# A hybrid Mamba-2 and attention trunk: step sizes by fp32 products, decay differences on ScalarE, sums in two half buffers

## The chip, the cores and the metric

The kernel runs on one core of a Trainium2 chip. The metric is the device time of one execution in microseconds. Engines are named as in the profile: PE (TensorE products) and PEld (its weight loads), DVE (VectorE), ACT (ScalarE), POOL (GpSimd) and SP (SyncE, which issues most DMAs).

## The reference, cut to what matters

The trunk has two layers on x of 256 tokens by 2048 channels: a Mamba-2 SSD mixer, then sliding-window attention. All of it is float32. The change lies in the first mixer:

```python
zxbcdt = x @ w_in                      # 2048 x (4096 z + 6144 xbc + 64 dt)
xbc = silu(conv4(xbc) + conv_b)        # xs (64 heads x 64), B and C (8 groups x 128)
dt = softplus(dt_raw + dt_bias)        # one step size per token and head
a = -exp(a_log)
# chunks of 128 tokens; s is the running sum of dt * a
y = sum over t <= q of (C[q] . B[t]) * exp(s[q] - s[t]) * (xs[t] * dt[t]) + xs * d_skip
y = rmsnorm_by_group(y * silu(z)) * norm_w
x = layernorm(alpha * x + y @ w_out)   # then the attention layer on this x
```

## The kernel before, in words

**Splits.** A float32 product on PE is made of three products of split halves: each weight block is loaded raw (`wr`), ACT writes its rounded half `wh` (L133), DVE the rest `wl` (L134), and PE adds wh·xH, wh·xL and wl·xH (L195 to L197, `mac`). x is split in the same way into xH and xL. A block ("unit") is 2048 by 128 weights, loaded as two halves of 512 KB; five raw buffers and four of each split half stand in turn, and loading runs two units ahead (`next_unit`, L179). In the SSD layer a block's 48 products of 128x128 by 128x256 fill one PSUM tile `mm` of four.

**Order of the work.** SSD heads go in eight groups. A group has ten projection blocks: B, C, four of xs, four of z (group 0 takes z first). Output products of the group before are put between them. A plan (`at`, L581 on) hangs the other steps behind a block number: `load_decay`, `sum_decay`, `exp_decay`, `cb` (C·B and the mask, multiplied into the decays), `tr` (transposes of xs), `ymm` (products with the decays), `gate`, `norm`. A scheduler then settles the order on each engine's queue, in which instructions stay in order; some steps get a priority (`high_priority`).

**The start.** `load_first` (L136) loads eight pieces of 1 to 3 k-tiles of 512 columns: 256 of x, 128 of the step-size block, 128 of block 0 (z). The step-size weights stand there twice, so that rows 0 to 63 and 64 to 127 of the product are the same 64 heads. `gemm_ws` (L282) makes both products, piece by piece. `make_dt` (L299) turns the first into dt by a series on DVE, splits dt·a into a coarse part (rows 0 to 63) and a rest (rows 64 to 127), and runs both sums along the tokens in one scan (L326); the sums go to DRAM (`rscr`, L327). `turn_dt` transposes the sums and dt on PE (L333, L334).

**Decays.** `load_decay` (L366) reads four heads' coarse and low sums back, broadcast to all 128 partitions (`rb`, one buffer, two loads of 512 KB). `sum_decay` (L378) makes on DVE, for each head, coarse[q] − coarse[t] + low[q] in two ops (L384, 256 columns; L388, 128 columns), then one minimum with 80 over all four heads (L392). `exp_decay` (L395) is one exp on ACT (L397). The low sum of t goes into dt (`dtx`). `ymm` (L453) multiplies the decays with xd on PE (L468: fp32, 64 columns, two halves of the array) and DVE adds xs·d_skip straight from PSUM (L475).

Of the kernel before, what the change touches and what calls it, by code (L numbers as in the profile page):

```python
# [28 lines left out]
NFIRST = 2  # L29
FIRST = [(0, 1), (1, 2), (2, 4), (4, 6), (6, 9), (9, 12), (12, 14), (14, 16)]  # L30
# [27 lines left out]
def trunk(ctx: ExitStack, tc: tile.TileContext, A: dict, out: bass.AP, dbg=None):  # L58
# [60 lines left out]

    def load_unit(src, places):  # L120
        u = new_unit(places)
        raws = []
        for c in range(2):
            raw = wp.tile([P, 1024], F32, tag="wr", name=nm("wr"), bufs=NR)
            nc.sync.dma_start(raw[:], src[:, c * 1024 : (c + 1) * 1024])
            raws.append(raw)
        for c in range(2):
            for (h, k0, k1), (l, _, _) in zip(*u.parts):
                a, b = max(k0, 8 * c), min(k1, 8 * c + 8)
                if a < b:  # L130
                    sl = slice((a - k0) * P, (b - k0) * P)
                    raw = raws[c][:, (a - 8 * c) * P : (b - 8 * c) * P]
                    nc.scalar.activation(h[:, sl], raw, AF.Copy)  # L133
                    nc.vector.tensor_tensor(l[:, sl], raw, h[:, sl].bitcast(F32), ALU.subtract)  # L134
        return u

    def load_first():

        us = [new_unit([WHOLE, WHOLE]) for _ in range(2)]
        for k0, k1 in FIRST:  # L140
            n = k1 - k0
            if n < 3:
                raw = wp.tile([P, 2, 512], F32, tag="wr", name=nm("first"), bufs=NR)
            else:
                raw = ap.tile([P, 3, 512], F32, tag="e", name=nm("first"), bufs=2)
            raw = raw[:, :n, :]
            nc.sync.dma_start(raw, A["first"][:, k0:k1, :])
            nc.scalar.activation(xH(k0, k1), raw[:, :, :S], AF.Copy)
            nc.vector.tensor_tensor(xL(k0, k1), raw[:, :, :S], xH(k0, k1).bitcast(F32), ALU.subtract)
            for i, u in enumerate(us):  # L150
                h, l = [p[:, k0 * P : k1 * P].rearrange("p (k c) -> p k c", c=P) for p in (u.h, u.l)]
                w = raw[:, :, S + i * P : S + (i + 1) * P]
                nc.scalar.activation(h, w, AF.Copy)  # L153
                nc.vector.tensor_tensor(l, w, h.bitcast(F32), ALU.subtract)
        return us


    srcs = [None]
# [20 lines left out]
    def next_unit():  # L179
        if not units:  # L180
            units.extend(load_first())
            nc.sync.dma_start(pc[:], A["pc"])
        while len(units) < min(used[0] + 1 + AHEAD, len(srcs)):
            if len(units) == 5:
                nc.sync.dma_start(cc[:], A["cc"])
            if len(units) in (8, 9):
                i = len(units) - 8
# [6 lines left out]
    def mac(ps, ah, al, bh, bl, first, last):  # L194
        nc.tensor.matmul(ps, ah, bh, start=first, stop=False)  # L195
        nc.tensor.matmul(ps, ah, bl, start=False, stop=False)  # L196
        nc.tensor.matmul(ps, al, bh, start=False, stop=last)  # L197
# [29 lines left out]
    class Split:  # L227


        def __init__(self, name, first, at0, at1):  # L230
            gap = (at1 - at0) % 256 // 4
            t = ap.tile([P, KT * S + 128], F32R, tag=name, name=name)
# [49 lines left out]
    def gemm_ws(us):  # L282
        pss = [mm_tile() for _ in us]
        for k0, k1 in FIRST:
            for ps, u in zip(pss, us):
                for k in range(k0, k1):
                    ks = slice(k * P, (k + 1) * P)
                    mac(
                        ps[:, :S], u.h[:, ks], u.l[:, ks], xH(k, k + 1)[:, 0, :], xL(k, k + 1)[:, 0, :],
                        k == 0, k == KT - 1,  # L290
                    )
        return pss
# [6 lines left out]
    def make_dt(ps):  # L299
        f = [ap.tile([P, S], F32, tag="sm", name=nm("f"), bufs=NSM) for _ in range(7)]  # L300
        u, e, rec, z, w, q, dt = [x[:] for x in f]
        nc.scalar.activation(u, ps[:, :S], AF.Identity, bias=pc[:, PC_DTB : PC_DTB + 1])
# [24 lines left out]
        nc.sync.dma_start(rscr[:], rc)  # L327
# [37 lines left out]

    def load_decay(g, hf):  # L366
        rb = ap.tile([P, 2, 4, S], F32, tag="rb", name=nm("rb"), bufs=1)
        h0 = g * 8 + hf * 4
        for part in range(2):
            nc.sync.dma_start(  # L370
                rb[:, part, :, :],
                rscr[part * 64 + h0 : part * 64 + h0 + 4, :]
                .rearrange("h q -> (h q)").partition_broadcast(P)
                .rearrange("p (h q) -> p h q", h=4),
            )
        rbs[g, hf] = rb

    def sum_decay(g, hf):  # L378
# [16 lines left out]
    def exp_decay(g, hf):  # L395
        e = es[g, hf]
        nc.scalar.activation(e[:], e[:], AF.Exp)  # L397
# [58 lines left out]
    def ymm(g):  # L456
        st = gs[g]
        st.yz = ap.tile([P, 4, S], F32, tag="yz", name=nm("yz"), bufs=1)
        for k in range(2):
            ps = ax_tile()  # L460
            for i in (2 * k, 2 * k + 1):
                o = (i % 2) * S
                xd = st.xd[i]
                for c in range(2):
                    cols = slice(o + c * P, o + S)
                    for r in range(2):
# [4 lines left out]
                        )  # L471
# [547 lines left out]
```

## Time and profile before

| | |
|---|---|
| runs, us | 1023.79, 1024.12, 1253.01 (median 1024.12) |
| profiled execution, us | 1023.71 |
| its span, us | 1021.9 |
| mean granted PE clock | 0.997 |
| busy PE / DVE / ACT / POOL, us | 1002.5 / 806.3 / 521.7 / 84.9 |
| DMA | 203.5 MB, 199 GB/s over the span |
| wh splits on ACT (L133), us | 338.0 |
| wl splits on DVE (L134), us | 393.5 |
| decay sums and minimum on DVE (L384, L388, L392), us | 36.2 + 24.5 + 15.2 |
| exp of decays on ACT (L397), us | 23.9 |
| landing of rb, median from issue, us | 4.8 |

Busy time is the union of an engine's instructions; a matmul's end is modelled and matmuls overlap, so the distance between the starts of two of them tells more than their durations. A row of a group gives busy time, mean duration, then the idle time of the engine just before, and who ended it. Names read out<-in, and shapes partitions by elements.

### The profile page before, as it was taken

Reading aid. Unit: us, or ns where it says so; the run is one execution under the profiler, and the core shown is the slowest. Engines: PE = TensorE matmul, PEld = TensorE weight load, DVE = VectorE, ACT = ScalarE, POOL = GpSimd, SP = SyncE. Lnnn points to the kernel's source line nnn. Section 1 sums busy time; section 2 is a strip of 40 time slices with the busy share of each in tenths; the row PEclk is TensorE's granted clock in tenths of the full one; section 3 lists DMA queues with packets and bytes.
Section 4 is the critical chain, followed back from the end, with each engine's and each line's share of the span. In section 5 each row is a group of like instructions: output and inputs, shape, how many; then the busy total and the mean of one; then the engine's idle time right before and its main releaser. Section 6 shows DMA issues by size and latency. Waiting matters only on the chain. (4 is left out here: it accounts for less than half of the span.)

```text
span 1021.9 us, 17613 instructions
## 1 busy us (share of the span) xinstructions
PE 1002.5 (98%) x7028; PEld 906.6 (89%) x7028; DVE 806.3 (79%) x1234; ACT 521.7 (51%) x795; POOL 84.9 (8%) x112
## 2 busy tenths in 40 slices
PE   7999999999999999999999999999999999999997
PEld 7998999999998998999999999878988878879975
DVE  6889897886895995986897797798577785785776
ACT  6565554744654554564464474535545453453642
POOL 0000303003003001100300300301000000000002
PEclk9999999999999999999999999999999999999999
DMA  8887585674764765666567466646555445545522
GB/s 307 281 301 241 167 270 176 226 235 141 260 212 143 266 202 192 213 208 219 178 207 239 159 196 229 241 145 234 195 167 170 154 142 182 173 142 182 193 97 82
DMA packets 55730, 203.50 MB, mean 199 GB/s; under 512 B 6288, under 2 KB 6560, under 8 KB 54880
## 3 DMA queue, kind: packets, MB, share of 16 engines
q1 hardware_dynamic: 54288, 196.33, 57.2%
q0 software_dynamic: 1072, 5.53, 1.6%
q8 instruction: 55, 0.90, 0.4%
q10 hardware_dynamic: 288, 0.52, 0.1%
q14 instruction: 27, 0.22, 0.1%
HBM read 200.13 MB, written 2.23 MB: 198 GB/s over the span
## 5 line engine op out<-in xcount | busy, mean ns | idle before, releaser
L134 DVE TENSOR_TENSOR wl<-wr,wh 128x1024 fp32r<-128x1024 f32 (+2 forms) x342 | 393.5, 1169 | 103.0 <-ACT wh L133 101.5
L133 ACT ACTIVATE wh<-wr 128x1024 fp32r<-128x1024 f32 (+2 forms) x342 | 338.0, 1012 | 230.8 <-PE mm L196 67.2
L195 PE MATMUL mm<-xH,wh 128*128 128x256 f32 x1296 | 361.7, 279 | 7.8 <-ACT wh L153 6.0
L197 PE MATMUL mm<-xH,wl 128*128 128x256 f32 x1296 | 360.3, 278 | 3.1 <-DVE wl L134 3.1
L196 PE MATMUL mm<-xL,wh 128*128 128x256 f32 x1296 | 360.7, 279 | 0.0
L195 PEld LDWEIGHTS mm<-xH,wh 128*128 128x128 f32 x1296 | 245.3, 189 | 9.8 <-ACT wh L153 6.3
L197 PEld LDWEIGHTS mm<-xH,wl 128*128 128x128 f32 x1296 | 245.2, 189 | 3.6 <-DVE wl L134 3.5
L196 PEld LDWEIGHTS mm<-xL,wh 128*128 128x128 f32 x1296 | 245.4, 189 | 1.1
L255 PE MATMUL mm<-wh,yH 128*128 128x512 f32 x256 | 101.4, 396 | 0.0
L256 PE MATMUL mm<-wh,yL 128*128 128x512 f32 x256 | 99.9, 390 | 0.0
L257 PE MATMUL mm<-wl,yH 128*128 128x512 f32 x256 | 99.7, 390 | 0.0
L482 POOL TENSOR_TENSOR yz<-yz,z 128x256 f32<-128x256 f32 x32 | 29.8, 931 | 538.5 <-DVE yz L475 538.5
L195 PE MATMUL mm<-x1H,wh 128*128 128x256 f32 x256 | 71.9, 281 | 0.0
L197 PE MATMUL mm<-x1H,wl 128*128 128x256 f32 x256 | 71.0, 277 | 0.0
L196 PE MATMUL mm<-x1L,wh 128*128 128x256 f32 x256 | 71.0, 277 | 0.0
L356 DVE SCALAR_TENSOR_TENSOR cv<-mm,pc,cv 128x255 f32<-128x255 f32 x144 | 68.6, 476 | 2.5 <-ACT cv L354 1.6
L704 PE MATMUL mm<-wh,x1H 128*128 128x512 f32 x160 | 63.3, 396 | 0.0
L706 PE MATMUL mm<-wl,x1H 128*128 128x512 f32 x160 | 62.7, 392 | 0.2 <-DVE wl L134 0.2
L705 PE MATMUL mm<-wh,x1L 128*128 128x512 f32 x160 | 62.7, 392 | 0.2 <-DVE x1L L668 0.2
L255 PEld LDWEIGHTS mm<-wh,yH 128*128 128x128 f32 x256 | 48.1, 188 | 10.3 <-DVE z L421 0.9
L257 PEld LDWEIGHTS mm<-wl,yH 128*128 128x128 f32 x256 | 48.1, 188 | 10.1
L256 PEld LDWEIGHTS mm<-wh,yL 128*128 128x128 f32 x256 | 48.1, 188 | 9.0
(181 smaller groups left out, 1308.5 us busy)
## 6 DMA issues: line engine op xcount, KB each, us to landing
wr<-in_wa SPq DMA_DIRECT2D x158, 512.0 KB, 5.2
wr<-in_wo SPq DMA_DIRECT2D x64, 512.0 KB, 5.3
rb<-rscr SPq DMA_DIRECT2D x32, 512.0 KB, 4.8
wr<-in_wq SPq DMA_DIRECT2D x32, 512.0 KB, 4.5
wr<-in_wg SPq DMA_DIRECT2D x32, 512.0 KB, 5.3
wr<-in_wb SPq DMA_DIRECT2D x32, 512.0 KB, 4.6
wr<-in_wkv SPq DMA_DIRECT2D x8, 512.0 KB, 6.6
first<-in_first SPq DMA_DIRECT2D x4, 512.0 KB, 8.8
```

Source lines behind the costliest of these rows:

```text
L133: nc.scalar.activation(h[:, sl], raw, AF.Copy)
L134: nc.vector.tensor_tensor(l[:, sl], raw, h[:, sl].bitcast(F32), ALU.subtract)
L195: nc.tensor.matmul(ps, ah, bh, start=first, stop=False)
L196: nc.tensor.matmul(ps, ah, bl, start=False, stop=False)
L197: nc.tensor.matmul(ps, al, bh, start=False, stop=last)
L255: nc.tensor.matmul(ps[:], aH[:, k, hs], u.h[:, ks], start=k == 0, stop=False)
L256: nc.tensor.matmul(ps[:], aL[:, k, hs], u.h[:, ks], start=False, stop=False)
L257: nc.tensor.matmul(ps[:], aH[:, k, hs], u.l[:, ks], start=False, stop=k == 3)
L356: nc.vector.scalar_tensor_tensor(a[:, sft:], ps[:, : S - sft], w(3 - sft), a[:, sft:], ALU.mult, ALU.add)
L704: nc.tensor.matmul(ps[:], x1H[:, kk, hs], u.h[:, ks], start=kk == 0, stop=False)
L705: nc.tensor.matmul(ps[:], x1L[:, kk, hs], u.h[:, ks], start=False, stop=False)
L706: nc.tensor.matmul(ps[:], x1H[:, kk, hs], u.l[:, ks], start=False, stop=kk == KT - 1)
```

## The change

Four things are altered.

1. The step sizes come from 16 fp32 products of 64 columns, straight from the raw pieces, with no split. Even k go to PSUM rows 0 to 63, odd k to rows 64 to 127; `make_dt` adds the two halves with two ACT copies across partitions and one DVE op. The pieces hold 448 columns. Block 1 is loaded in two halves among the pieces, and products of the step sizes and blocks 0 and 1 are pinned to the order in `ORDER`. Raw pieces are now read by PE too, so their buffers come free later; the last one borrows a buffer of `rb`.
2. The decay differences are made on ACT: Relu(coarse[t] − coarse[q]), and the exp takes them with scale −1. The minimum on DVE is gone.
3. The low sum of q is left out of the difference. Its exp is taken once in `make_dt`, stored, loaded for a group as `el` (two loads of 64 partitions), and multiplied on DVE into ymm's result (128x512), before xs·d_skip is added in SBUF.
4. `rb` is two buffers of half the size, with only the coarse sums, and the plan loads both halves together; sums and exps stand at other block numbers. The pc scaling goes behind `make_dt`.

```diff
+FIRST = [(0, 1), (1, 2), (2, 4), (4, 6), (6, 8), "h0", (8, 11), (11, 14), (14, 16), "h1"]
+ORDER = [(0, 0, 1), (1, 0, 2), (0, 1, 4), (1, 2, 6), (0, 4, 8), (1, 6, 8), (2, 0, 8), (0, 8, 14), (1, 8, 14),
+         (0, 14, 16), (1, 14, 16), (2, 8, 16)]
+FW = 256 + 128 + 64
...
+        for piece in FIRST:
+            if isinstance(piece, str):
+                c = int(piece[1])
+                split_half(us[1], load_half(us[1], A["wa"][1], c), c)
+                continue
...
+            if k0 == 14:
+                raw = ap.tile([P, 4 * S], F32, tag="rb", name=nm("first"), bufs=2)
+            elif n < 3:
+                raw = wp.tile([P, 1024], F32, tag="wr", name=nm("first"), bufs=NR)
             else:
-                raw = ap.tile([P, 3, 512], F32, tag="e", name=nm("first"), bufs=2)
+                raw = ap.tile([P, 1536], F32, tag="e", name=nm("first"), bufs=2)
...
+    def first_products():
+        us, raws = load_first()
+        units.extend(us)
+        nc.sync.dma_start(pc[:], A["pc"])
+        pss = [mm_tile() for _ in range(3)]
+        for i, k0, k1 in ORDER:
+            if i:
+                narrow(pss[i], us[i - 1], k0, k1, True)
+                continue
+            for k in range(k0, k1):
+                r = 64 * (k % 2)
+                tc.keep_in_program_order(
+                    nc.tensor.matmul(
+                        pss[0][r : r + 64, :S], raws[k][:, S + P :], raws[k][:, :S], start=k < 2, stop=k >= KT - 2
+                    )
                 )
...
-        nc.scalar.activation(u, ps[:, :S], AF.Identity, bias=pc[:, PC_DTB : PC_DTB + 1])
+        for r in (0, 64):
+            nc.scalar.copy(e[r : r + 64], ps[64 - r : 128 - r, :S])
+        nc.vector.scalar_tensor_tensor(u, ps[:, :S], pc[:, PC_DTB : PC_DTB + 1], e, ALU.add, ALU.add)
...
-        nc.sync.dma_start(rscr[:], rc)
+        nc.sync.dma_start(rscr[0:64, :], rc[:64])
+        nc.scalar.activation(hi[64:128], rc[64:128], AF.Exp)
+        nc.sync.dma_start(rscr[64:128, :], hi[64:128])
...
     def load_decay(g, hf):
-        rb = ap.tile([P, 2, 4, S], F32, tag="rb", name=nm("rb"), bufs=1)
+        rb = ap.tile([P, 4, S], F32, tag="rb", name=nm("rb"), bufs=2)
...
+    def load_low(g):
+        el = ap.tile([P, 4, S], F32, tag="el", name=nm("el"), bufs=1)
+        rows = rscr[64 + g * 8 : 64 + g * 8 + 8, :].rearrange("(i r) q -> r i q", r=2)
+        for r in range(2):
+            nc.sync.dma_start(el[64 * r : 64 * r + 64, :, :], rows[r].partition_broadcast(64))
+        els[g] = el
...
         for h in range(4):
-            nc.vector.scalar_tensor_tensor(
-                e[:, h, :256], rb[:, 0, h, :], rtk[:, 0, h0 + h : h0 + h + 1], rb[:, 1, h, :],
-                ALU.subtract, ALU.add,
-            )
-            nc.vector.scalar_tensor_tensor(
-                e[:, h, 256:], rb[:, 0, h, 128:], rtk[:, 1, h0 + h : h0 + h + 1], rb[:, 1, h, 128:],
-                ALU.subtract, ALU.add,
-            )
-        nc.vector.tensor_scalar(e[:], e[:], 80.0, None, ALU.min)
+            for c, cols in ((0, slice(0, 256)), (1, slice(256, 384))):
+                nc.scalar.activation(
+                    e[:, h, cols], rb[:, h, c * P :], AF.Relu, scale=-1.0, bias=rtk[:, c, h0 + h : h0 + h + 1]
+                )
...
-        nc.scalar.activation(e[:], e[:], AF.Exp)
+        nc.scalar.activation(e[:], e[:], AF.Exp, scale=-1.0)
...
+            two = slice(2 * k, 2 * k + 2)
+            nc.vector.tensor_tensor(
+                st.yz[:, two, :], ps[:].rearrange("p (i q) -> p i q", i=2), els[g][:, two, :], ALU.mult
+            )
             for i in (2 * k, 2 * k + 1):
-                o = (i % 2) * S
                 col = PC_D + g * 4 + i
-                nc.vector.scalar_tensor_tensor(
-                    st.yz[:, i, :], st.xs[i][:], pc[:, col : col + 1], ps[:, o : o + S], ALU.mult, ALU.add
-                )
+                v = st.yz[:, i, :]
+                nc.vector.scalar_tensor_tensor(v, st.xs[i][:], pc[:, col : col + 1], v, ALU.mult, ALU.add)
...
-            at(t - 5, load_decay, g, 0)
-            at(t - 1, sum_decay, g, 0)
-            at(t - 1, load_decay, g, 1)
-            at(t + 1, sum_decay, g, 1)
-            at(t + 2, exp_decay, g, 0)
-            at(t + 2, exp_decay, g, 1)
+            at(t - 5, load_decay, g, 0)
+            at(t - 5, load_decay, g, 1)
+            at(t, load_low, g)
+            steps = t - 1
...
+        at(steps, sum_decay, g, 0)
+        at(steps + 1, exp_decay, g, 0)
+        at(steps + 1, sum_decay, g, 1)
+        at(steps + 2, exp_decay, g, 1)
```

More of the change, by code (lines that the diff above doesn't have):

```diff
@@ L118, in new_unit, with load_half, split_half @@
         return u
+    def load_half(u, src, c):
+        raw = wp.tile([P, 1024], F32, tag="wr", name=nm("wr"), bufs=NR)
+        nc.sync.dma_start(raw[:], src[:, c * 1024 : (c + 1) * 1024])
+        return raw
+    def split_half(u, raw, c):
+        for (h, k0, k1), (l, _, _) in zip(*u.parts):
+            a, b = max(k0, 8 * c), min(k1, 8 * c + 8)
+            if a < b:
+                sl = slice((a - k0) * P, (b - k0) * P)
+                v = raw[:, (a - 8 * c) * P : (b - 8 * c) * P]
+                nc.scalar.activation(h[:, sl], v, AF.Copy)
+                nc.vector.tensor_tensor(l[:, sl], v, h[:, sl].bitcast(F32), ALU.subtract)
     def load_unit(src, places):
         u = new_unit(places)
-        raws = []
+        raws = [load_half(u, src, c) for c in range(2)]
         for c in range(2):
[L124 to L134, printed above, removed]
+            split_half(u, raws[c], c)
         return u
@@ L192, in next_unit, with mac @@
         return units[used[0] - 1]
[L194 to L197, printed above, removed]
+    def mac(ps, ah, al, bh, bl, first, last, pin=False):
+        for a, b, i in ((ah, bh, 0), (ah, bl, 1), (al, bh, 2)):
+            m = nc.tensor.matmul(ps, a, b, start=first and i == 0, stop=last and i == 2)
+            if pin:
+                tc.keep_in_program_order(m)
     pending = []
@@ L364, in trunk @@
     es = {}
+    els = {}
     def load_decay(g, hf):
[L367 removed]
+        rb = ap.tile([P, 4, S], F32, tag="rb", name=nm("rb"), bufs=2)
         h0 = g * 8 + hf * 4
[L369 to L374, printed above, removed]
[L375 to L376 removed]
+        nc.sync.dma_start(
+            rb[:],
+            rscr[h0 : h0 + 4, :]
+            .rearrange("h q -> (h q)").partition_broadcast(P)
+            .rearrange("p (h q) -> p h q", h=4),
+        )
+        rbs[g, hf] = rb
+    def load_low(g):
[4 more added lines that the diff above has]
+        els[g] = el
     def sum_decay(g, hf):
```

85 lines of the change are left out of this document (37 added, 48 removed).

## The prediction

> **What bounds the kernel now.** I read the page first, then the table by stretch of time, then PE's waits, then the timelines around the two places where PE stops. Times are us from the span's start.
>
> ```profile
> span 1021.9 us, 17613 instructions
> PE 1002.5 (98%) x7028; PEld 906.6 (89%) x7028; DVE 806.3 (79%) x1234; ACT 521.7 (51%) x795; POOL 84.9 (8%) x112
> ```
>
> ```profile
> 0.00:27.40 27.40, 20.56 (x144) 19.86 (x145) 17.86 (x36) 18.51 (x36) 0.30 (x5) 1.00 0.84 298
> 27.40:78.10 50.70, 50.70 (x441) 50.24 (x440) 42.51 (x76) 30.33 (x37) 0.31 (x1) 1.00 0.84 297
> 78.10:87.90 9.80, 7.50 (x52) 7.29 (x51) 9.15 (x12) 3.54 (x6) 0.00 (x0) 0.83 0.55 175
> 87.90:640.00 552.10, 550.28 (x4255) 518.12 (x4255) 454.99 (x687) 289.20 (x377) 63.59 (x83) 1.00 0.63 208
> ```
>
> Columns are length, busy PE, PEld, DVE, ACT, POOL, granted PE clock, DMA share, GB/s. PE is the bound: from 87.9 to 640 it is idle for 1.8 of 552 us. Only two stretches have slack, the start (6.8 us idle) and 78.1 to 87.9 (2.3 idle, and a clock of 0.83). An engine that is merely relieved brings nothing elsewhere. PE's waits and timeline name the stops:
>
> ```profile
> PE mm L195 <- ACT wh L153: 6.0, 2, 4.3
> PE mm L197 <- DVE wl L134: 3.1, 2, 2.3
> PE mm L195 <- DVE cv L356: 1.8, 2, 1.2
> ```
>
> ```profile
> 13.25 0.28 PE L195 MATMUL mm<-xH,wh 128*128 128x256 f32 x1
> 13.37 0.28 PE L196 MATMUL mm<-xL,wh 128*128 128x256 f32 x1
> ...
> 25.03 0.39 PE L197 MATMUL mm<-xH,wl 128*128 128x256 f32 x1 [0.82 <-DVE wl L134]
> ...
> 80.99 0.39 PE L197 MATMUL mm<-xH,wl 128*128 128x256 f32 x1 [2.30 <-DVE wl L134]
> ```
>
> A projection product is issued every 0.114 us (13.25 to 13.37), while before 13.1 the same rows stand 0.213 apart: the clock starts at half. In the start PE waits twice for the splits of the first pieces (4.29 until its first product, then 6.86 to 9.00) and at 23.93 for a wl half. The stop at 78.41 is the dearest: the next product starts 2.58 later, and then they stand 0.213 apart until 84.8, so that the block's 48 products take from 78.18 to 87.83, 9.65 instead of 48 x 0.114 = 5.47. It costs **4.2 us**. DVE shows why:
>
> ```profile
> 75.66 1.75 DVE L433 TENSOR_TENSOR e<-e,cbm 128x1536 f32<-128x1536 f32 x1
> 77.32 0.48 DVE L356 SCALAR_TENSOR_TENSOR cv<-mm,pc,cv 128x253 f32<-128x253 f32 x1
> 77.71 1.75 DVE L433 TENSOR_TENSOR e<-e,cbm 128x1536 f32<-128x1536 f32 x1
> 79.38 0.42 DVE L360 SCALAR_TENSOR_TENSOR xs<-xs,cv 128x256 f32<-128x256 f32 x1
> 79.71 1.22 DVE L134 TENSOR_TENSOR wl<-wr,wh 128x1024 fp32r<-128x1024 f32 x1
> ```
>
> The split that PE wants stands last in a DVE queue which, from 55 on, has also run group 0's 16 decay sums (L384, L388) and two minima (L392). The first of them began at 55.24, behind the landing of rb.
>
> **The change, part by part.**
>
> *Step-size product.* Removed: 48 split products. Six run before the stop at 6.86. Of the 42 after 9.00, 12 are at half clock and 30 at full: 12 x 0.213 + 30 x 0.114 = 6.0. Added: 16 fp32 products of 64 columns on raw pieces. The nearest row is ymm's (same shape, fp32):
>
> ```profile
> 99.84 2.82 PE L468 MATMUL ax<-e,xd 128*64 128x256 f32 x32
> 102.59 0.39 PE L195 MATMUL mm<-xH,wh 128*128 128x256 f32 x1
> ```
>
> Those 32 records are 16 products of two passes each. A pass of 256 columns takes 0.216, and the two column halves start 0.007 apart, so a pair costs 0.43, and a product alone the same. Entering and leaving such a run costs 0.09 + 0.21 (0.205 instead of 0.114 ahead; 0.202 and 0.223 instead of 0.102 and 0.114 behind). In the new order k0, k1 and the pair k2, k3 read pieces as they land, while the split products still wait for ACT (a piece's first ACT op starts at 8.01, its first product at 9.00): free, hidden by the two early stops. k4 to k7 are two pairs at half clock, 1.72. k8 to k15 are four pairs, 1.72. Three excursions x 0.30 = 0.9. Together 4.3, net **-1.6**. If the halves didn't overlap, k4 to k15 would cost 8 x 0.43 + 4 x 0.86 + 0.9 = 7.8, net +1.8.
>
> The Trainium skill's TensorEngine Tiling, section Tiling Modes, says that a change of tiling mode drains TensorE. That speaks against alternating the two kinds five times; the 0.30 above is what the trace shows of it, and without it the net would be -2.5.
>
> *Delivery.* The pieces carry 448 columns instead of 512, and block 1 comes as two halves between them: 4.5 MB for three blocks instead of 5. The trace's pieces are taken up at 8.01 (fourth k), 11.12 (ninth), 12.97 (twelfth): 0.42 MB a us. The last half lands near 16.8 and its wl is done near 19.3 (ACT 1.05, DVE 1.22 and a short queue). PE needs it at about 21.5 by its own pace, so PE and not delivery sets the end. SP is passed by the h0 load, which waits for piece 0's buffer (its split ends at 4.9, its fp32 product before); three pieces stand behind it, but 1.8 MB are queued ahead, six us of transfer. At 23.93 PE waits now because DVE does a reciprocal (1.75) ahead of a half of that block; in the new order h1's wl and three further halves stand ahead of it: **-1.0**. The bound by delivery alone (19.3 + 24 x 0.114 = 22.0 instead of 27.3) is -5.3. The start in sum: **-2.6**, the third block ending at 24.7, not 27.3.
>
> *make_dt.* Two ACT copies and one DVE op of about 0.4 replace one ACT op. The scan stands behind the cv of the fifth block (due at 24.7 + 3 x 5.47 = 41.1), so it ends near 42.8. Its reader, the transposes on PE, come at 24.7 + 4 x 5.47 = 46.6. Hidden, 3.8 spare; before it was 4.7 (44.6 to 49.3).
>
> *Decay sums to ACT.* DVE loses 36.2 + 24.5 + 15.2 (L384, L388, L392) and gains 16 products of 128x512 from PSUM (0.68 as at L264: 10.9); the four D terms a group stay (L475, 0.48). Net -65 of 806. ACT gains 64 x 0.50 + 64 x 0.39 by L815's rows (bias per partition, SBUF): 57 at most, 522 to 579. Neither is the bound; what counts is the queues.
>
> The Trainium skill, ScalarE: Activation LUTs, Rules for kernel authors, says to give relu, min and add to VectorE; by its figure of 280 ns + 0.833 a column, less 93 of overlap, ACT would gain an estimated 44. The rule prices an engine's time; here DVE's is dearer, so it moves no term of the sum.
>
> At 78: the 16 sums and two minima (16 x 0.33 + 2 x 0.87 = 7 us of DVE starts) leave the queue ahead of the wl at 79.71, which was 2.3 late. Now ACT: behind rb's wait stand eight Relus (2.9), cv, exp (1.5), xs and the wh of a second half. Scan 42.8, store to landing 1.7, then wr, rb, rb, el, el are issued ahead of that half's wr. rb took 1.3 to 3.5 each (before: 51.67, 55.12, 63.03, 65.75), so they land near 48.5, 51 and 53.5, the half's wr near 55; ACT finishes it at 57, DVE at 58. PE asks for it six blocks, the transposes and half a block on: 24.7 + 6 x 5.47 + 0.9 + 2.7 = 61.1. So 3 spare, and the next halves have more. The stop at 78 goes with its half-clock window: **-4.2**; bounds 0 and -4.2. What is late next is the cb step (below).
>
> *Later groups.* ACT holds 16 Relus, two exps and four yH ops right behind ymm: 8 x 0.89 + 2 x 1.5 + 4 x 0.5 = 12. The wh behind them is wanted three blocks and an output unit later (3 x 5.47 + 5.45 = 21.8). Cost 0, 8 spare with its own two splits; without that cover each group would pay the difference. el waits on SP for ymm's DVE op, with wr loads behind; these are for blocks 30 us on: 0. The stops at 201.54 and 283.87 (0.93 and 1.44, excess 2.1; PE waits for a PSUM buffer that cv frees between two e*cbm of 1.75) keep their DVE order: taken 0, bounds 0 and -2.1.
>
> **Sum.** The profiled execution took 1023.71 (span 1021.9), 0.4 under the median of 1024.12. 1023.7 - 1.6 - 1.0 - 4.2 = 1016.9, so **1017**.
>
> **Rivals.**
> - *The start gives nothing back.* Half clock lasts longer: it ended at 13.1 after PE had been busy from 9.00, and fell again from 81.4 to 84.8 after a stop of 2.3. A gap between 9.7 and 13.1 would leave it at half until 16.5, +1.7. With the pairs not overlapping (+3.4) the start is +2.5: 1023.7 + 2.5 - 4.2 = 1022.0; with the clock alone 1018.6. Against it: PE has two landed pieces queued then. The Trainium skill, TensorE: Matmul & The Clock Gate, Part 1, calls the window free-running, 3.4 us long, and needs one busy window; the trace agrees (81.4 to 84.8 is one).
> - *The stop at 78 moves to ACT.* If rb lands as late as before (55.1), the Relus end near 58, the half's wl at 61 to 62, PE stops for a moment or pays a half-clock window of 1.7 as well: 1023.7 - 2.6 - 1.5 = 1019.6 to 1022.
> - *Slower.* ACT becomes the pace-setter at each change of group: the queue of 12 behind ymm must grow to over 20, for instance by Relu at twice L815's time plus rb late. From there each us counts in seven groups; 2 us give 1016.9 + 14 = 1031. ACT at 51% speaks against it.
> - *More than forecast.* Delivery bound and cb stops gone: 1023.7 - 5.3 - 4.2 - 2.1 = 1012.1.
>
> **How the numbers follow.** Forecast 0.6 (1014 to 1019); start gives nothing 0.13 (1018.6 to 1022); stop moves 0.15 (1019.6 to 1022); slower 0.07 (above 1024); more than forecast 0.05 (1012). The range 1012 to 1022.5 holds them but for the slower case and the edges. Two per cent, about what a measurement of this kernel can tell from no change, is 20.5 us, three times the forecast gain: faster 0.02, same 0.95, slower 0.03 (the far end of the ACT case).
>
> **What would show it.** Step-size products: pairs about 0.43 apart at full clock, third block ending at 24 to 25.5. Stop: no PE gap over 0.5 between 30 and 100, clock 1.00 there. ACT: Relus near 0.5 and 0.39, no PE wait for ACT wh. DVE near 740 busy, ACT near 575. Wrong would be a PE wait for wh or wl in 55 to 75, or small repeated waits in each group behind ymm.

## The result, and the profile after

The changed kernel takes 1019.84 us (median of 5 runs, 1019.52 to 1023.16), against 1024.12 for the kernel before: the ratio is 0.9967 [0.9954, 0.9981]. One of the five executions of the kernel before took 1253.01 and has no part in the ratio. The profiled execution took 1019.52 with a span of 1017.7, so it is compared with the 1023.71 and 1021.9 of the profile before. The interval of the ratio lies below 1, so the gain is real. It is 4.2 us between the two profiled executions and 3.4 by the ratio, where 7 were forecast.

The engines' lines of the page after:

```profile
span 1017.7 us, 17576 instructions
PE 1001.8 (98%) x7012; PEld 900.8 (89%) x7012; DVE 772.2 (76%) x1099; ACT 560.5 (55%) x917; POOL 89.8 (9%) x112
```

PE is the bound as before. The table by stretch shows where it is idle (the columns are length, busy PE, PEld, DVE, ACT, POOL, granted PE clock, DMA share and GB/s):

```profile
0.00:23.93 23.93, 19.76 (x128) 15.32 (x129) 12.70 (x24) 14.09 (x27) 0.30 (x5) 1.00 0.89 332
60.00:63.00 3.00, 1.85 (x14) 1.45 (x13) 1.49 (x2) 3.00 (x7) 0.00 (x0) 1.00 0.95 388
119.00:122.00 3.00, 2.10 (x13) 1.59 (x13) 3.00 (x7) 1.75 (x4) 0.00 (x0) 1.00 0.69 214
278.00:280.00 2.00, 1.07 (x10) 0.91 (x9) 2.00 (x3) 1.99 (x3) 0.00 (x0) 1.00 0.07 29
280.00:640.00 360.00, 360.00 (x2766) 338.66 (x2766) 273.37 (x362) 202.41 (x303) 45.01 (x54) 1.00 0.61 196
```

The clock column reads 1.00 for the start too, although products stand 0.213 apart there until 9.8; in the start the spacing tells more than the column. The stop at 78 and its stretch at a clock of 0.83 are gone. In their place are a stop at 60 to 62, with DMA at 388 GB/s, and one at 120. PE's waits name them, and one more in front of the layer norm (L702). The second wait for wl is in the start, at 12.7; the two for cv are at 120 and 279:

```profile
PE mm L208 <- DVE cv L389: 1.8, 2, 0.9
PE mm L208 <- DVE wl L136: 1.5, 2, 0.8
PE ax L702 <- DVE xr L697: 1.5, 2, 1.2
```

The most useful reading of two such traces is a difference of starts: PE runs the same sequence of steps in both, so the start of a step after, minus its start before, is the lead at that point, and a jump in the lead is a place where time came or went. (Lead in us, negative is ahead; the starts are in the two timelines.)

| step on PE | before | after | lead | what lies between |
|---|---|---|---|---|
| transposes of dt | 49.31 | 45.88 | -3.42 | the start |
| cb of group 0 | 66.70 | 64.99 | -1.71 | new stop at 60 to 62 |
| tr of group 0 | 93.42 | 87.72 | -5.70 | old stop at 78 is missing |
| tr of group 1 | 131.13 | 126.58 | -4.56 | new stop at 120 |
| tr of group 2 | 218.94 | 213.50 | -5.44 | old stop at 201 is missing |
| tr of group 3 | 301.77 | 296.10 | -5.68 | |
| norm of the last group | 653.39 | 647.52 | -5.87 | |
| transposes of the layer norm | 671.73 | 667.03 | -4.70 | new stop at 665 |
| span | 1021.9 | 1017.7 | -4.2 | a half-clock window at 1010 |

So the change earned 3.4 at the start, 4.0 at 78 and 0.9 at 201, and three new stops gave back 1.7, 1.1 and 1.2.

### The profile page after: what moved, and what is told of

It reads as the page before. It is cut to its first block, busy times and chain, and to the rows that moved or that the text cites. A ratio compares the mean times of both kernels' runs of the same rounds, so it can differ in the third digit from the quotient of the medians.

```text
span 1017.7 us, 17576 instructions
## 1 busy us (share of the span) xinstructions
PE 1001.8 (98%) x7012; PEld 900.8 (89%) x7012; DVE 772.2 (76%) x1099; ACT 560.5 (55%) x917; POOL 89.8 (9%) x112
## 4 chain that ended last, share of the span: by engine, by line
PE 77%; DVE 9%; ACT 5%; DMA 5%; issue 3%; POOL 1%; SPq 0%; ACTq 0%; DVEq 0%; POOLq 0%
PE mm L208 40%; PE mm L268 7%; PE mm L269 7%; PE mm L270 7%; PE mm L744 3%; PE mm L745 3%; PE mm L746 3%; DVE wl L136 3%; ACT wh L135 2%; DMA wr<-in_wa 2%; DVE cv L389 1%; PE ax L506 1%; DMA rb<-rscr 1%; PE ax L836 1%; PE ax L883 1%
## 5 line engine op out<-in xcount | busy, mean ns | idle before, releaser
L136 DVE TENSOR_TENSOR wl<-wr,wh 128x1024 fp32r<-128x1024 f32 (+2 forms) x342 | 398.3, 1181 | 132.3 <-ACT wh L135 131.1
L208 PE MATMUL mm<-xH,wh 128*128 128x256 f32 x1280 | 356.6, 279 | 2.2 <-DVE cv L389 1.8
L208 PE MATMUL mm<-xH,wl 128*128 128x256 f32 x1280 | 355.0, 277 | 1.5 <-DVE wl L136 1.5
L208 PE MATMUL mm<-xL,wh 128*128 128x256 f32 x1280 | 354.9, 277 | 0.0
L208 PEld LDWEIGHTS mm<-xH,wh 128*128 128x128 f32 x1280 | 241.0, 188 | 6.8 <-issue 2.6
L208 PEld LDWEIGHTS mm<-xH,wl 128*128 128x128 f32 x1280 | 240.9, 188 | 2.1 <-DVE wl L136 1.9
L208 PEld LDWEIGHTS mm<-xL,wh 128*128 128x128 f32 x1280 | 241.1, 188 | 0.9
L522 POOL TENSOR_TENSOR yz<-yz,z 128x256 f32<-128x256 f32 x32 | 32.9, 1037 | 523.3 <-DVE yz L517 523.3
```

Of the source, the lines that this page charges most:

```text
L136: nc.vector.tensor_tensor(l[:, sl], v, h[:, sl].bitcast(F32), ALU.subtract)
L208: m = nc.tensor.matmul(ps, a, b, start=first and i == 0, stop=last and i == 2)
L522: nc.gpsimd.tensor_tensor(v, v, st.z[i][:], ALU.mult)
```

## Experiments

Times in one set are medians beside runs of the kernel before on the same chip (1024.08, 1024.34 and 1024.58 in the three sets of four). Single runs of one kernel spread by 3 to 8 us in most sets, so verdicts rest on the leads in the traces where the medians lie close.

**The start alone.** Edit: the changed start, with the decays put back.

```diff
-                nc.scalar.activation(e[:, h, cols], rb[:, h, c * P :], AF.Relu, scale=-1.0, bias=...)
+            nc.vector.scalar_tensor_tensor(e[:, h, :256], rb[:, 0, h, :], rtk[...], rb[:, 1, h, :],
+                ALU.subtract, ALU.add)
...
+        nc.vector.tensor_scalar(e[:], e[:], 80.0, None, ALU.min)
```

> The changed start (step sizes by fp32 products on raw pieces, order pinned) with the decays of the kernel before (sums and minima on DVE, one rb buffer with both parts, no el). My theory: start and stop are independent terms. The start alone gives its 3.4 us at the transposes of dt, and the stop near 75 to 80, in which PE waits for DVE wl behind the decay sums, stays at 4 or more, with a half-clock window behind it: about 1020.5 us (1019.8 to 1021.5). Rival: the two are not independent. If the lead of the start only moves PE nearer to the late splits, the stop grows by the lead and the total is that of the kernel before, 1023 to 1024.

Measured: 1020.08, ratio 0.9959 [0.9945, 0.9974]. The lead at the transposes of dt is 3.17, and the stop is there:

```profile
78.12 0.39 PE L208 MATMUL mm<-xH,wl 128*128 128x256 f32 x1 [2.60 <-DVE wl L136]
```

```profile
74.00:79.00 5.00, 2.40 (x21) 2.20 (x20) 5.00 (x6) 2.30 (x4) 0.00 (x0) 1.00 0.02 9
79.00:82.00 3.00, 3.00 (x28) 3.00 (x28) 3.00 (x5) 0.17 (x1) 0.00 (x0) 1.00 0.71 244
```

The second fence has the stretches around it. The wait of 2.60 is longer than the 2.30 of the kernel before, and yet the clock stays at 1.00 behind it. So the half-clock window, 1.7 of the forecast's 4.2 (half of the time from 81.4 to 84.8), need not come with the stop. And the start alone is as fast as the whole change (0.9967), so as placed the decays brought nothing measurable on top of it.

**The decays alone.** Edit: the start of before, the decays of after (and 64 columns less behind xH and xL in SBUF).

> The start of the kernel before (step sizes by split products) with the changed decays (ACT Relus, el, exponentials of the low part stored). My theory: the stop at 78 (4.2) and the one at 201 (0.9) go; the stop that the changed kernel has at 60 to 61 (1.7) is there too, since SP issues its wr loads behind the scan and behind rb and el in both, and the scan moves with the start; the loss of 1.2 in front of the layer norm stays. Sum: 1019.5 minus the missing 3.4 of the start, 1022 to 1023.2. Rival: the stop at 60 comes only because PE is ahead by the start's lead; then it is missing here and the total is 1020 to 1021.5.

Measured: 1022.12, ratio 0.9984 [0.9974, 0.9995]. The stops at 62.3 and 63.5 (0.9 each), at 124.9 and at 670 are there although PE is not ahead at the transposes of dt (50.45, against 49.31 before); the rival falls. The new stops belong to the decays.

**Group 0's el loads three blocks later.**

```diff
-            at(TS, load_low, 0)
+            at(TS + 3, load_low, 0)
```

> The changed kernel with one edit: group 0's two el loads are put into SP's order three blocks later, behind the wr loads instead of ahead of them. My theory: the stop at 60.4 and 61.3 (1.7 together) is SP's order: the wr that PE's block waits for is issued behind rb, rb, el, el, and lands at 59.8. With el behind it, it lands 2.5 earlier and the stop is gone or under 0.3: 1017.6 to 1018.4 us, with the lead over the kernel before near 5 at 65 us. Rival A: ACT is what is late (its queue of Relus behind rb's landing at 56.5); then the stop stays as it is and the total is that of the changed kernel, 1019.5. Rival B: the stop at 119.7, or the clock window it would take, takes the gain back later: gain at 65 us, 1019 at the end.

Measured: 1020.96, ratio 0.9975 [0.9961, 0.9989]; in the trace no stop between 25 and 119, and a lead of 6.27 at tr of group 0, although this execution ran at half clock from 10.5 to 13.9 (lead 2.09 at the transposes of dt). The wr behind rb lands at 56.37, not 59.78. This run alone doesn't settle the stop at 60, since PE also comes 1.34 later than in the changed kernel; the kernel with three edits (below) does. The lead was lost again in front of the layer norm, where PE waits 3.04 and then runs a window at half clock. The forecast total (1018) was a miss, the place was right.

**The differences back on DVE.**

```diff
-                nc.scalar.activation(e[:, h, cols], rb[:, h, c * P :], AF.Relu, scale=-1.0, bias=rtk[...])
+                nc.vector.tensor_scalar(e[:, h, cols], rb[:, h, c * P :], rtk[...], 0.0, ALU.subtract, ALU.min)
...
-        nc.scalar.activation(e[:], e[:], AF.Exp, scale=-1.0)
+        nc.scalar.activation(e[:], e[:], AF.Exp)
```

> The changed kernel with the decay differences back on DVE, one tensor_scalar (subtract, min 0) for each Relu on ACT, and the exponential without its scale of -1; the el split stays. DVE gains 64 x about 0.29 and 64 x about 0.2 (31 us of 772), ACT loses about 46. My theory: moving the differences to ACT is not what removes the stop at 78; halving the sums (no minimum, one operand) and ending the double rb buffer wait is. Then no stop comes back at 78, the stop at 119.7 (ACT behind its queue) goes, and the stop at 60 is there or smaller: 1018 to 1019.5 us. Rival: DVE's queue is what matters, and with 16 differences in front of wl the stop at 78 returns, with a half-clock window: 1021 to 1024.

Measured: 1019.95, ratio 0.9961 [0.9948, 0.9975], equal to the changed kernel. At 76.05 PE stops for 0.5 only, so it was not the move to ACT that removed the stop at 78. At 61 it stops for 0.3; PE comes 0.65 later here and the wr lands at 58.30. The stop at 119.7 is there all the same (0.71 of wait for cv), so my reading of it, ACT's longer queue of Relus, falls.

**The gb loads on SP.**

```diff
-        nc.gpsimd.dma_start(gb[:, 0, :], A["lng"][0].partition_broadcast(P))
+        nc.sync.dma_start(gb[:, 0, :], A["lng"][0].partition_broadcast(P))
```

(and the same for the second half)

> The changed kernel with the two broadcast loads of the first layer norm (gb, 2 MB) issued by SP, where they come behind the last wo loads and two wkv loads, instead of by POOL. My theory: the 1.2 that are lost in front of the layer norm (PE's stop at 665.5) come from the last wo load, issued 0.6 behind gb and landing at 649.9 behind its 2 MB. Without gb ahead it lands about 3.6 after its issue at 642.3, near 646; ACT takes it 4 earlier, and PE's stop at 665 shrinks from 1.55 to under 0.5: 1018.3 to 1018.9 us, the lead over the kernel before at the transposes staying near 5.9. Rival: the load is late because it is issued late (its buffer is freed 4 later after ymm than before); then it lands at 649 all the same and the time is that of the changed kernel, 1019.5 to 1020.

Measured: 1017.19, ratio 0.9936 [0.9916, 0.9956]. The wo load that goes out next to gb, the last but one of wo, is what matters here (the expectations call it the last). In the changed kernel ACT and PE show it late (first fence); in this one ACT waits only for its buffer and the transposes for nothing (second):

```profile
650.00 1.06 ACT L135 ACTIVATE wh<-wr 128x1024 fp32r<-128x1024 f32 x1 [5.88 <-DMA wr<-in_wo]
652.37 0.26 ACT L550 ACTIVATE r<-ax,eps_t 128x2 f32<-128x2 f32 x1
...
667.03 0.63 PE L702 MATMUL ax<-cc,xr 128*128 128x128 f32 x4 [1.16 <-DVE xr L697]
```

```profile
649.12 1.06 ACT L135 ACTIVATE wh<-wr 128x1024 fp32r<-128x1024 f32 x1 [3.43 <-PE mm L269]
651.50 0.26 ACT L550 ACTIVATE r<-ax,eps_t 128x2 f32<-128x2 f32 x1
...
667.45 0.63 PE L702 MATMUL ax<-cc,xr 128*128 128x128 f32 x4
```

The load is issued at 643.87 and lands at 647.32, 3.5 later; in the changed kernel it was issued at 642.29, 0.6 behind the second half of gb, and landed at 649.89, 7.6 later. In the kernel before it went out at 644.10, ahead of gb at 646.93, and took 3.5. With gb on SP the lead is 4.29 at the norm of the last group and 4.28 at the transposes: nothing is lost between. So the cost is the order of two issues, on two different engines. The other traces agree. In the seven profiles where this load stands behind gb it takes 7.60 to 9.48 us, and PE's wait is 1.16 to 3.04, the load's time less 6.3 to 6.5 in each; where it goes out ahead of gb it takes 3.5 to 3.7, and PE doesn't wait. The wait of 3.04 in the kernel with later el loads belongs to the slowest of these loads (9.48). The Trainium skill, DMA: Bandwidth & Descriptors, section "Issuing engines are not separate DMA queues", says that loads issued by different engines interleave on the same 16 DMA engines; the 7.6 here agrees.

**The products by el left out.** (The low part of the decay is missing from the result.)

```diff
-            nc.vector.tensor_tensor(
-                st.yz[:, two, :], ps[:].rearrange("p (i q) -> p i q", i=2), els[g][:, two, :], ALU.mult
-            )
...
-                nc.vector.scalar_tensor_tensor(v, st.xs[i][:], pc[:, col : col + 1], v, ALU.mult, ALU.add)
+                nc.vector.scalar_tensor_tensor(v, st.xs[i][:], pc[:, col : col + 1], ps[:, o : o + S],
+                    ALU.mult, ALU.add)
```

> The changed kernel without the products by el (the low part of the decay is left out of the result; el is loaded, and the D term reads PSUM again). It prices what the factored low part adds behind ymm. My theory: 16 products of 0.68 and the D terms' and yL's longer durations (0.695 and 0.794 instead of 0.475 and 0.525) go, 24 to 26 us of DVE, and the chain from ymm to the first gate is back at 3.2 from 4.4; with it the stop at 119.7 (1.3) goes and so does the loss in front of the layer norm, 1017.5 to 1018.5 us. Rival: the D terms and yL stay long, since they are slowed by POOL's gates and not by the product, and the stop at 119.7 stays because it is ACT's exponential that holds cv back: 1019 to 1020.

Measured: 1019.35, ratio 0.9952 [0.9937, 0.9966]. The first POOL gate is back at 3.18 behind ymm's start (4.37 in the changed kernel), that wo load goes out at 640.20, ahead of gb, and the stop in front of the layer norm is gone: the longer chain behind ymm is what made that load late. The stop near 120 stays, and is longer (1.52 of wait): not the product's doing, and with it the forecast total was missed. At 61 PE waits only 0.3, although its instructions up to there are those of the changed kernel: it comes to the transposes of dt 0.8 later, and the wr lands at 59.30. So the size of that stop hangs on PE's lead as well as on SP's order. The D terms and yL, in groups by line, in the changed kernel and in this one:

```profile
L537 DVE SCALAR_TENSOR_TENSOR yL<-yz,pc,yH 128x256 fp32r<-128x256 f32 x32 | 24.8, 794 | 9.4 <-ACT yH L536 9.4
L517 DVE SCALAR_TENSOR_TENSOR yz<-xs,pc,yz 128x256 f32<-128x256 f32 x32 | 20.5, 695 | 0.0
```

```profile
L536 DVE SCALAR_TENSOR_TENSOR yL<-yz,pc,yH 128x256 fp32r<-128x256 f32 x32 | 18.9, 594 | 24.1 <-ACT yH L535 24.1
L514 DVE SCALAR_TENSOR_TENSOR yz<-xs,pc,ax 128x256 f32<-128x256 f32 x32 | 13.4, 477 | 0.0
```

**One rb buffer, differences on DVE.**

```diff
-        rb = ap.tile([P, 4, S], F32, tag="rb", name=nm("rb"), bufs=2)
+        rb = ap.tile([P, 4, S], F32, tag="rb", name=nm("rb"), bufs=1)
```

> The kernel with the differences on DVE (the one before of my experiments on that) with one half-size rb buffer instead of two: the second half's load waits until the first half's differences are done. My theory: the stop at 78 of the kernel before is the wait for the second rb, in DVE's queue ahead of the split, more than DVE's work: with one buffer a stop of 1.5 or more returns between 72 and 80. Time 1021 to 1023. Rival: the number of sums and minima was what mattered; then the stop at 76 stays at 0.5 as with two buffers, and the time at 1020.

Measured: 1020.74, ratio 0.9976 [0.9958, 0.9994]; no stop at all between 25 and 118, and a lead of 7.09 at tr of group 0. My theory, the wait for the second rb, falls. With one buffer SP issues the second rb behind a wr, and that wr lands at 57.81 (58.30 with two buffers and the differences on DVE, 59.78 in the changed kernel); two buffers let SP put 0.5 MB more ahead of what PE wants next. In group 1 the second rb lands at 114.10, and its differences run from 114.13 to 116.4, ahead of three splits and three cv operations; PE waits 2.37 for the last cv.

**Three edits together**: el later, gb on SP, and group 1's second exponential one block later.

```diff
-        at(steps + 2, exp_decay, g, 1)
+        at(steps + (3 if g == 1 else 2), exp_decay, g, 1)
```

> The changed kernel with three edits at places far apart: group 0's el loads three blocks later, the gb loads on SP, and group 1's second exponential one block later. My theory: the stops at 60 (1.5), 119.7 (1.1) and 665 (1.2) are three separate queue orders, so their gains add up: lead over the kernel before of about 6 at 66, 7 at 130, 8 at the transposes of the layer norm; 1015.5 to 1016.5 us. Rivals: the second exponential only swaps places with the split that PE wants next, and the stop at 119 moves to 122 (1 less gain); or the gain in front of the layer norm is taken by the transposes waiting for the factor r behind its two table loads (1 to 2 less): 1017.5 to 1019.

Measured: 1016.91, ratio 0.9929 [0.9912, 0.9946]; span 1013.3. Leads: 7.45 at tr of group 0, 8.34 at tr of group 2, 8.62 at the transposes of the layer norm. The transposes of dt come at 45.84, as early as in the changed kernel, and there is no stop at 60: the wr behind rb lands at 54.76, not 59.78. That settles SP's order as the cause of that stop. The stop at 120 is gone too. DVE's timeline shows how: in the changed kernel a wl whose wh stood on ACT behind the exponential comes first, and each of the three cv operations, of which the last frees PE's PSUM buffer, stands behind a split (first fence). Here two cv run as soon as ACT's part is done, with one split among them (second):

```profile
116.22 1.23 DVE L136 TENSOR_TENSOR wl<-wr,wh 128x1024 fp32r<-128x1024 f32 x1 [1.10 <-ACT wh L135]
117.36 0.48 DVE L389 SCALAR_TENSOR_TENSOR cv<-mm,pc,cv 128x255 f32<-128x255 f32 x1
117.75 1.22 DVE L136 TENSOR_TENSOR wl<-wr,wh 128x1024 fp32r<-128x1024 f32 x1
118.89 0.48 DVE L389 SCALAR_TENSOR_TENSOR cv<-mm,pc,cv 128x254 f32<-128x254 f32 x1
119.28 1.21 DVE L136 TENSOR_TENSOR wl<-wr,wh 128x1024 fp32r<-128x1024 f32 x1
120.41 0.47 DVE L389 SCALAR_TENSOR_TENSOR cv<-mm,pc,cv 128x253 f32<-128x253 f32 x1
```

```profile
114.94 1.00 DVE L389 SCALAR_TENSOR_TENSOR cv<-mm,pc,cv 128x255 f32<-128x255 f32 x2 [0.42 <-ACT cv L387]
115.89 1.22 DVE L136 TENSOR_TENSOR wl<-wr,wh 128x1024 fp32r<-128x1024 f32 x1
117.03 0.47 DVE L389 SCALAR_TENSOR_TENSOR cv<-mm,pc,cv 128x253 f32<-128x253 f32 x1
```

The last cv ends 3.4 earlier (117.50 against 120.88), of which 1.75 is PE's own lead over the changed kernel there. ACT's own part of cv comes no earlier against PE than in the changed kernel (114.36 against 116.09); what the exponential held up was the wh and, through DVE's queue, the cv operations behind its wl.

**Both parts loaded, half the sum's work.** The start alone, with this in place of the sums and minima (the low part is loaded, but missing from the result):

```diff
+                nc.vector.tensor_scalar(e[:, h, cols], rb[:, 0, h, c * P :], rtk[...], 0.0,
+                    ALU.subtract, ALU.min)
```

> The changed start with the decays of the kernel before, of which one half of the work is left out: both parts of rb are loaded into the one buffer as before, but each difference is one tensor_scalar on the high part alone, and the minimum over the whole tile is gone (the low part is missing from the result). It asks what made the stop near 75 to 78: DVE's work on the sums (7 us a group, here about 3.6) or the second rb, of twice the bytes, landing at 63. If DVE's work: no stop over 0.5 near 75, and the lead over the kernel before at 93 is 6.5 to 7. If the landing: the stop stays at 2 or more and the lead at 93 is 4 to 5. I take the first, since the kernel with one half-size rb buffer had no stop there.

Measured: 1015.00, ratio 0.9904 [0.9882, 0.9925]. No stop near 75, and a lead of 7.30 at tr of group 0:

```profile
74.00:79.00 5.00, 5.00 (x46) 5.00 (x46) 5.00 (x7) 2.88 (x4) 0.00 (x0) 1.00 0.65 220
```

The bytes are those of before, in one buffer; only DVE's work is shorter. It acts in two ways that this run doesn't part: the split stands behind less work, and the one buffer is free earlier (the second rb pair is issued at 54.2, not 57.6 as with the start alone). Fewer bytes, a second buffer and the move to ACT are not needed for the stop at 78 to go. Which part of the shorter sum does it, the missing operand or the missing minimum, wasn't parted either.

**The step-size product in two runs instead of five.**

```diff
-ORDER = [(0, 0, 1), (1, 0, 2), (0, 1, 4), (1, 2, 6), (0, 4, 8), (1, 6, 8), (2, 0, 8), (0, 8, 14), (1, 8, 14),
-         (0, 14, 16), (1, 14, 16), (2, 8, 16)]
+ORDER = [(1, 0, 2), (1, 2, 6), (1, 6, 8), (0, 0, 8), (2, 0, 8), (1, 8, 14), (1, 14, 16), (0, 8, 16), (2, 8, 16)]
```

> The changed kernel with the fp32 step-size products in two runs (k0 to k7 and k8 to k15, each behind the split products) instead of five. My theory: the early products on raw pieces are free and also begin PE's busy time at 3.4 instead of 4.9; in two runs they save three excursions of 0.30 but lose the free places of k0 to k3 (0.9 to 1.7): the transposes of dt come 0 to 1 later than in the changed kernel (45.9 to 47 at the same phase of the clock), total 1019.5 to 1021. Rival: excursions and mixing cost more than the filling brings; then the transposes come before 45.5.

Measured: 1024.14, ratio 0.9994 [0.9982, 1.0006]; the transposes of dt come at 53.30. Both expectations missed the wait that decides:

```profile
13.56 1.03 PE L315 MATMUL mm<-first 128*64 128x256 f32 x8
18.50 0.39 PE L207 MATMUL mm<-xH,wh 128*128 128x256 f32 x1 [3.91 <-ACT wh L134]
```

h0's load waits for piece 0's buffer, which is free only when k0's fp32 product has run; it is issued at 13.32 here, at 4.56 in the changed kernel. So the early products are not only filling: they free the buffer of the third block's load. It also shows what a lead is worth: this execution is 7.4 later than the changed kernel at the transposes (1.7 of it a half-clock window from 19.4 to 22.8), 5.5 later at tr of group 0 and 3.6 in the profiled time, since the stops at 60 and 120 are missing here.

**A fourth edit**: group 3's second product of e by cbm two blocks later.

```diff
+        if g == 3:
+            at(t + pos["cb"] + 2, times_cb, g, 1)
```

> The kernel with three edits and one more: in group 3 the second product of e by cbm (1.75 on DVE) runs two blocks later, so that the cv operations of the next block have one long product less among them. My theory: the stop at 275.5 (1.05), where PE waits for the PSUM buffer that the last cv frees, is DVE's order alone; it goes, and the time is 1 less than with three edits: profile near 1014 with the same clock windows, median 1015.5 to 1016.5. Rival: the two xr products at 276.5 and the split behind them then come first on DVE and PE waits for a split instead: no gain.

Measured: 1014.93, ratio 0.9912 [0.9891, 0.9933], faster than both kernels. Against three edits (0.9929) the intervals overlap, so what the fourth brings by itself isn't shown by the times. In the trace the stop at 275 is gone; one of 0.9 at 75 came in this execution. What PE still waits for most:

```profile
PE mm L316 <- DMA first<-in_first: 3.5, 1, 3.5
PE mm L208 <- DVE wl L136: 1.4, 2, 0.7
PE ax L876 <- DVE o L896: 1.0, 1, 1.0
```

**The changed kernel again, unedited.**

> The changed kernel once more, unedited, beside the others: it shows what differs between two profiles of the same instructions. Expected: the stops at 60 to 61, 119.7, 278 and 665 again, within 0.5 each, since they are queue orders; a stop near 77, which the kernel with gb on SP had and the changed kernel did not although their instructions are the same up to there, would show that this one hangs on when a load lands; and the half-clock window at 1010 need not come again. Median 1019.5 to 1020.5.

Measured: 1021.65, ratio 0.9971 [0.9955, 0.9986]. The stops at 60, 120, 279 and 666 are there again. One near 76 (0.9) is new: ACT waits for a load issued at 68.05 that lands at 74.36, where it took from 68.39 to 73.87 in the first profile. The median is above the one expected. The wait at 666 was 2.33, not within 0.5 of the 1.16 in the first profile, and was followed by products 0.43 apart:

```profile
668.73 0.96 PE L702 MATMUL ax<-cc,xr 128*128 128x128 f32 x4 [2.33 <-DVE xr L697]
669.34 0.78 PE L268 MATMUL mm<-wh,yH 128*128 128x512 f32 x1
669.91 0.63 PE L269 MATMUL mm<-wh,yL 128*128 128x512 f32 x1
670.34 0.63 PE L270 MATMUL mm<-wl,yH 128*128 128x512 f32 x1
```

So two profiles of the same instructions differ by 2.8 us in span, mainly by one such load, one longer wait and where the windows of the clock fall.

## Where the prediction was right, and the step that failed

*Step-size product and delivery (forecast -2.6): about right, and luck on top.* The forecast kept the clock of the profile before, whose products stand 0.213 apart until 13.1. Three executions with the new start came near that: they were full at 12.9, 11.4 and 11.2 (differences on DVE, without products by el, one rb buffer) and lead by 2.63 to 2.91 at the transposes. A microsecond at half clock costs half of itself, so at the clock of before their leads would be an estimated 1.8 to 2.7. The fp32 products behave as priced:

```profile
16.19 1.51 PE L316 MATMUL mm<-first 128*64 128x256 f32 x12
19.89 0.65 PE L316 MATMUL mm<-first 128*64 128x256 f32 x4
```

Three pairs from 16.19 to the next split product at 17.63 are 1.44 (forecast 3 x 0.43 + 0.3 = 1.59), and the last half of block 1 landed at 16.98 (forecast 16.8). A wait of 0.8 for h0's split (12.44 to 13.47) was not foreseen. The lead of 3.4 in the changed kernel's profile is larger than forecast because the clock rose sooner: by the spacing of the products it was full between 8.6 and 9.9 in seven of the eleven profiles with this start, with leads of 3.1 to 3.6. The forecast did not have this; what makes it rise sooner no run here shows. (The eleventh, with el later, was full at 9.9, at half clock again to 13.9, and led by 2.09.)

*The stop at 78 (forecast -4.2): it went, but the step "3 spare" failed.* Between 66.7 and 93.4 the profile gained 4.0, as priced. What failed is the landing of the loads ahead of it: "the half's wr near 55; ACT finishes it at 57, DVE at 58", and with PE asking at 61.1, "3 spare". It landed at 59.78, ACT finished at 61.05 and PE took the split at 62.36. This is the PE wait "for wh or wl in 55 to 75" that the prediction itself named as a sign of being wrong. SP's queue, ACT's split of that wr, and PE:

```profile
44.16 0.52 SPq L357 DMA_DIRECT2D rscr<-f  x1
45.38 0.46 SPq L360 DMA_DIRECT2D rscr<-f  x1
45.88 0.58 SPq L126 DMA_DIRECT2D wr<-in_wa  x1
46.56 0.87 SPq L404 DMA_DIRECT2D rb<-rscr  x2
47.53 1.41 SPq L417 DMA_DIRECT2D el<-rscr  x2
48.99 1.40 SPq L126 DMA_DIRECT2D wr<-in_wa  x2
```

```profile
60.01 1.04 ACT L135 ACTIVATE wh<-wr 128x1024 fp32r<-128x1024 f32 x1
```

```profile
60.44 0.28 PE L208 MATMUL mm<-xH,wl 128*128 128x256 f32 x1
61.10 0.39 PE L208 MATMUL mm<-xH,wh 128*128 128x256 f32 x1 [0.39 <-ACT wh L135]
61.33 0.28 PE L208 MATMUL mm<-xL,wh 128*128 128x256 f32 x1
62.36 0.39 PE L208 MATMUL mm<-xH,wl 128*128 128x256 f32 x1 [0.76 <-DVE wl L136]
```

ACT started that split 0.23 after the landing, so it was the load that was late, and not ACT's queue. The loads landed one behind the other, at 51.29 (wr), 52.74, 56.45 (rb), 57.50, 58.80 (el) and 59.78. The first rb is 4.2 later than my 48.5. Of these, 1.6 are the store, which landed at 46.11 instead of 44.5. The other 2.6 are the first load behind it: I allowed 4.0 from the store's landing to the first rb, with a wr ahead of it. In the profile before, the first rb alone took 5.4 from its issue (46.31 to 51.67); here the wr in front took 5.4 (45.88 to 51.29), and the rb landed 6.6 behind the store. That lost 1.7. It is the rival "the stop at 78 moves to ACT", nearly to its numbers (wl at 61 to 62, total 1019.6 to 1022), to which I gave 0.15, though ACT's queue was not what delayed it.

There was luck in the 4.0 as well. Of the 4.2, 1.7 are a half-clock window that does not follow each such stop: the start alone had a wait of 2.60 without one, the changed kernel's second profile a wait of 2.33 with one. Against the profile before, the decays are worth 2.3 from the transposes of dt to tr of group 0 in the first profile and 1.65 in the second, and the start alone, whose stop had no window behind it, gains 1.1 there.

*What removed the stop.* I put it down to sums leaving DVE for ACT. The runs say that the shorter sum (one operand, no minimum) does it on either engine; what is left at 75 to 77 is nothing in some profiles and a stop of 0.5 to 1.2 in others. In the changed kernel's second profile it is a late load.

*Later groups (forecast 0, 8 spare): failed in group 1.* I asked when PE wants the wh behind ACT's queue, and not what stands on DVE behind the wl that waits for that wh: the cv operations that free a PSUM buffer. It cost 1.1.

*In front of the layer norm: not in the prediction.* I let the D terms stay at 0.48 and looked at no queue behind the last ymm. There the product and the longer D terms delay the gates by 1.2, and that moved a wo load behind gb. It cost 1.2 in the first profile and up to 3.0 in others, with the time that this load took.

*201 and 283 (taken 0): the first went (0.9), the second stayed.* This is inside the bound of 2.1; why the first went was not tested.

*Engine times.* ACT 560.5 was near (575): the Relus stand 0.35 apart on average where they follow each other. DVE is 772.2, not 740: I added durations that overlap (16 x 0.33 + 2 x 0.87 = 7 a group is 56, not 76), and the means of the D terms and of yL grew by 0.22 and 0.27, 32 of each, 15.6 together.

Sum of what was measured, by the table of leads: -3.4 (start) + 1.7 (stop at 60) - 4.0 (78) + 1.1 (120) - 0.9 (201) - 0.4 (to the norm of the last group) + 1.2 (layer norm) + 0.5 (the end) = -4.2.

## What to carry to other kernels

When a change puts loads ahead of another, write down their landings as one line that starts when the queue is free, and follow the wanted load to its end; issue-to-landing times of single loads hide that line. A lead won early is kept only where what PE waits for later moves with it: compare the start of each step in the two traces, and look for the queue order behind each place where the lead shrinks. Three such orders, four lines of code, were worth about as much here as the change itself (ratios to the kernel before of 0.9929 with them, 0.9967 and 0.9971 without).

## What was not expected of the hardware

A DVE operation with both tensor operands in SBUF can be slower while POOL works beside it. In the changed kernel the D term took 0.472 at its shortest and 0.965 at its longest (mean 0.695): eight that had no POOL operation beside them took at most 0.475, and eight that had one all the time took 0.83 to 0.96. With PSUM as one operand it took 0.477 in the mean, with or without POOL beside it. POOL's work alone does not decide it: yL, which has both operands in SBUF and POOL beside it throughout, took 0.483 to 0.959 in the kernel before. The Trainium skill, SBUF — State Buffer, section "Who interferes with whom", says that a DVE instruction with two SBUF inputs contends with a GpSimd instruction that reads SBUF; the D terms agree.

The half clock does not follow from the length of a stop: of the five waits of PE over 2.2 behind the start, in all profiles, those of 2.30, 2.33 and 3.04 were followed by products at half speed, and those of 2.37 and 2.60 were not. The Trainium skill, TensorE: Matmul & The Clock Gate, Part 1, calls the window free-running and 3.4 us long; a draw by its phase agrees with these five, but no run here shows the phase itself.
